# Convolution taps taken in turns over two channel halves, and a new order for all five engines

## The chip, the cores and the metric

One core of one Trainium2 chip runs the whole program. The metric is the device time in microseconds (us) of one execution; of several runs the median is taken. Names used below: PE is TensorE's matmul (PEld its weight load), DVE is VectorE, ACT is ScalarE, POOL is GpSimd, SP is SyncE, which issues most DMAs here.

## The reference

Two layers over 256 tokens of width 1024, float32. Each layer normalises `x`, multiplies it by one wide input matrix, and feeds three groups whose outputs are joined and multiplied by an output matrix:

```
h = rms_norm(x, norm_g);  z = h @ w_in             # 1024 -> 3612 columns
o_a = fox_attention(q, k, v, f_logit) * silu(f_gate)      # 4 heads, forget bias
y   = a * sigmoid(b)                                       # GLU, 256 channels
y   = causal depthwise conv(y, 31 taps) + conv_b
o_b = (silu(layer_norm(y)) @ w_pw) * silu(c_gate)
o_c = nsa_attention(...) * silu(n_gate)                    # 8 heads, 3 branches
x   = x + concat(o_a, o_b, o_c) @ w_out
```

A final RMSNorm follows. The compressed branch of `nsa_attention` gathers blocks of 32 tokens, adds a position table, and sends them through a small two-layer network. What the change touches directly is the depthwise convolution: for each of 256 channels, 31 shifted copies of the sequence times a weight, summed.

## The kernel before, in words

Every float32 product that matters is split into a high and a low part: `form_hi` (ACT, line 227) rounds a 128x1024 piece of weights to the high part, `form_lo` (DVE, line 235) subtracts to get the low part and frees the raw buffer, whereupon SP may fetch the next piece (`pump`; six raw buffers). One input block of 128 columns, `s(i)`, is 24 matmuls on PE (lines 436 to 438), and two neighbouring blocks share one of two PSUM banks of the pool `z`: a block can only start when the bank's former contents have been read.

The 31 taps of the convolution are shared out. The last 11 (`NV`) are done on DVE by `late_taps`: the first is a multiply with bias (line 547), the other ten are `scalar_tensor_tensor` instructions (line 549) that read a shifted window of the padded input `ypad`, multiply by a per-channel weight and add to `yc`. The 256 channels are two halves of 128, so `yc[:, 0]` and `yc[:, 1]` are separate sums of 256 tokens each. The other 20 taps are matmuls: `glu` writes `ypad` (line 506), POOL sends it to a DRAM buffer and reads it back in the shape for matmuls (`yr`), `taps` (line 519) forms the weights and `conv` (line 529) runs 80 small matmuls into `pcn`; `conv_bias` (line 535) adds them to `yc`.

Names in the order of one layer that the prediction uses:

- `fox_kl` (line 707) writes `fklz`, which reads the PSUM bank of blocks 14 and 15 and feeds `fox_scores` (lines 717 and 718, tile `fs`); `fox_mask` (line 461) and `fox_exp` follow, `fox_norm` (lines 740 and 464, tiles `fsu`, `fP`) scales the rows, and `fox_trans` (line 748, tile `fpt`) transposes them on PE.
- `blocks(0)` and `blocks(1)` (line 818) write `xp` on DVE from the bank of blocks 0 and 1; `compress(0)` and `compress(1)` (line 828, tile `ph`) multiply `xp` by weights `ww` on PE.
- `keys_rope`, `keys_lo` (tile `klz`), `query_rope(0)` (tiles `q0r`, `q0u`) and `query` (tile `qs`) are DVE and ACT work that `scores` (tile `sw`) waits for.
- `fox_qh` and `fox_k0` (lines 681 and 695) are copies on POOL.
- `norms`, `trans`, `pv`, `proj1`, `residual` close a layer.

The order of every engine's instructions is the order of the calls in the text of the kernel: the whole program runs under a manual schedule for SP, PE, POOL, DVE and ACT, so that a call which stands later in the text stands later in the queue of each engine it uses, and an engine takes its queue strictly in order. The same list of calls is used for both layers.

Of the kernel before, what the change touches and what calls it, by code (L numbers as in the profile page):

```python
# [12 lines left out]
ALU = mybir.AluOpType  # L13
# [116 lines left out]
def trunk(ctx, tc, a, out, dbg=None):  # L130
# [243 lines left out]
    for l in range(L):  # L374
# [163 lines left out]

            ve.tensor_scalar(S("ct"), S("ct"), 0.5, None, op0=ALU.mult)

        def late_taps(i, a_, b_):

            ctv = S("ct").rearrange("p (i k) -> p i k", i=2)
            for k in range(a_, min(b_, NV)):
                y, w_ = ypad[:, i, 31 - NV + k:31 - NV + k + 256], ctv[:, i, k:k + 1]
                if k == 0:
                    ve.tensor_scalar(yc[:, i], y, w_, S("cb")[:, i:i + 1], op0=ALU.mult, op1=ALU.add)
                else:
# [612 lines left out]
            mprod(1, "A", NA)  # L1161
            a_out(1)
        form_hi()
        form_hi()
        form_lo()
        form_hi()
        form_lo()
        form_lo()
        mprod(1, "B", NB)
        b_out(1)  # L1170
        branch_gates()
        s(2)
        triangle()
        form_hi()
        form_lo()
        half_taps()
        s(3)
        glu_tanh(0)
        glu(0)
        forget()  # L1180
        form_hi()
        form_hi()
        late_taps(0, 0, 2)
        late_taps(0, 2, 4)
        late_taps(0, 4, 6)
        s(4)
        s(5)
        form_lo()
        form_lo()
        s(12)  # L1190
        forget_sum()
        cumulate()
        form_hi()
        form_lo()
        form_hi()
        s(13)
        glu_tanh(1)
        late_taps(0, 6, 8)
        glu(1)
        bias_rows()  # L1200
        late_taps(0, 8, 10)
        form_hi()
        form_hi()
        form_lo()
        form_lo()
        bias_heads()
        fox_q()
        s(14)
        s(15)
        fox_k()  # L1210
        s(6)
        form_lo()
        fox_qh()
        s(7)
        fox_k0()
        late_taps(0, 10, 12)
        late_taps(1, 0, 2)
        late_taps(1, 2, 4)
        form_hi()
        form_lo()  # L1220
        fox_kl()
        form_hi()
        form_lo()
        form_hi()
        form_lo()
        load_w2()
        keys_rope()
        fox_scores(0)
        fox_mask(0)
        form_hi()  # L1230
        form_lo()
        form_hi()
        taps(0)
        fox_scores(1)
        fox_scores(2)
        fox_mask(1)
        s(0)
        late_taps(1, 4, 6)
        s(1)
        fox_exp(0)  # L1240
        fox_exp(1)
        fox_scores(3)
        fox_mask(2)
        blocks(0)
        keys_hi()
        fox_exp(2)
        form_lo()
        s(8)
        taps(1)
        fox_mask(3)  # L1250
        s(9)
        fox_norm(0)
        keys_lo(0)
        query_rope(0)
        keys_lo(1)
        fox_exp(3)
        compress(0)
        part(0)
        blocks(1)
        conv(0)  # L1260
        conv(1)
        query(0, 0)
        compress(1)
        query(0, 1)
        fox_trans(0, 0)
        fox_trans(0, 1)
        fox_copy(0, 0)
        s(10)
        fox_norm(1)
        fox_trans(1, 0)  # L1270
        fox_copy(0, 1)
        late_taps(1, 6, 8)
        late_taps(1, 8, 10)
        late_taps(1, 10, 12)
        form_hi()
        form_lo()
        form_hi()
        form_lo()
        fox_trans(1, 1)
        scores(0)  # L1280
        mask(0, 0)
        part(1)
        fox_copy(1, 0)
        hidden()
        fox_copy(1, 1)
        fox_pv()
        s(11)
        mask(0, 1)
        expo(0, 0)
        expo(0, 1)  # L1290
        conv_bias(0)
        hidden_in()
        conv_bias(1)
        coeff(0)
        norms(0, 0)
        trans(0, 0)
        gelu()
        ln_trans()
        form_hi()
        form_hi()  # L1300
        form_hi()
        norms(0, 1)
        form_hi()
        form_hi()
        form_lo()
        query_rope(1)
        form_lo()
        scores(1)
        compressed_kv()
        compressed_v()  # L1310
        query(1, 0)
        query(1, 1)
        s(16)
        s(17)
        form_hi()
        mask(1, 0)
# [7 lines left out]
        trans(0, 1)
        form_lo()
        ln_norm()
        scores(2)
        mask(2, 0)
        expo(1, 1)
        coeff(1)  # L1330
        norms(1, 0)
        mask(2, 1)
        ptcopy(0)
        gate_tanh(0)
        scores(3)
        gate_mul(0)
        norms(1, 1)
        mask(3, 0)
        expo(2, 0)
        expo(2, 1)  # L1340
        coeff(2)
        norms(2, 0)
        norms(2, 1)
        compressed()
        form_lo()
        form_lo()
        s(19)
        s(20)
        gate_tanh(1)
        trans(1, 0)  # L1350
        trans(1, 1)
        ptcopy(1)
        expo(3, 0)
        scores(4, (0,))
        mask(3, 1)
        mask(4, 0)
        scores(4, (1,))
        mask(4, 1)
        ln_back()
        trans(2, 0)  # L1360
        s(21)
        expo(3, 1)
        scores(5, (0,))
        swish_in()
        trans(2, 1)
        ptcopy(2)
        cmp_scores(0)
        expo(4, 0)
        mixed(0, 2, fx["o"], 0.5)
        expo(4, 1)  # L1370
        gate_mul(1)
        swish()
        cmp_soft(0)
        scores(5, (1,))
        s(22)
        mask(5, 0)
        expo(5, 0)
        mask(5, 1)
        form_hi()
        form_hi()  # L1380
        form_lo()
        coeff(3)
        form_lo()
        norms(3, 0)
        norms(3, 1)
        pointwise()
        s(23)
        cmp_norm(0)
        coeff(4)
        trans(3, 0)  # L1390
        trans(3, 1)
        gate_tanh(2)
        gate_mul(2)
        scores(6, (0,))
        scores(6, (1,))
        scores(7, (0,))
        mix_hi(0, 2)
        mix_lo(0, 2)
        expo(5, 1)
        norms(4, 0)  # L1400
        norms(4, 1)
        ptcopy(3)
        pv(0)
        mask(6, 0)
        pv(1)
        coeff(5)
        pv(2)
        pv(3)
        gate_tanh(3)
        gate_mul(3)  # L1410
        scores(7, (1,))
        form_hi()
        form_hi()
        form_hi()
        cmp_scores(1)
        mixed(2, 2, ln["o"], 0.25)
        cmp_trans(0)
        cmp_copy(0)
        norms(5, 0)
        norms(5, 1)  # L1420
        proj0(0, (0, 1))
        form_lo()
        mix_hi(2, 2)
        mix_lo(2, 2)
        form_lo()
        trans(4, 0)
        ptcopy(4, 0)
        mask(6, 1)
        pv_cmp(0)
        trans(4, 1)  # L1430
        ptcopy(4, 1)
        proj0(0, (2, 3))
        mixed(4, 4, on[0], 0.5, TA)
        mix_hi(4, 4, TA)
        form_lo()
        load_g(a["norm_g"][1] if l == 0 else a["final_g"], nm("gn"))
        expo(6, 0)
        form_hi()
        mix_lo(4, 4, TA)
        trans(5, 0)  # L1440
        trans(5, 1)
        cmp_soft(1)
        proj0(0, (4, 5))
        proj0(0, (6, 7))
        form_lo()
        proj0(1, (0, 1))
        residual(0, 0, 512, pj[0])
        expo(6, 1)
        coeff(6)
        norms(6, 0)  # L1450
        norms(6, 1)
        ptcopy(5, 0)
        ptcopy(5, 1)
        mask(7, 0)
        proj1(range(4))
        form_hi()
        form_hi()
        mask(7, 1)
        expo(7, 0)
        expo(7, 1)  # L1460
        trans(6, 0)
        ptcopy(6, 0)
        trans(6, 1)
        ptcopy(6, 1)
        form_lo()
        form_lo()
        proj0(1, (2, 3))
        proj0(1, (4, 5))
        cmp_norm(1)
        cmp_trans(1)  # L1470
        form_lo()
        cmp_copy(1)
        proj0(1, (6, 7))
        coeff(7)
        norms(7, 0)
        norms(7, 1)
        trans(7, 0)
        ptcopy(7, 0)
        trans(7, 1)
        ptcopy(7, 1)  # L1480
        pv(4)
        pv(5)
        pv(6)
        pv(7)
        residual(0, 512, 512, pj[1])
        nxt.squares(0)
        nxt.rms(0)
        form_hi()
        pv_cmp(1)
        mixed(4, 2, on[1][:, 0:2], 0.5, TB)  # L1490
        form_lo()
        form_lo()
        mix_hi(4, 2, TB)
        mixed(6, 2, on[1][:, 2:4], 0.5, TB)
        mix_hi(6, 2, TB)
        mix_lo(4, 2, TB)
        mix_lo(6, 2, TB)
        proj2(0)
        proj1(range(4, 8))
        form_hi()  # L1500
# [79 lines left out]
```

## Time and profile before

| | us |
|---|---|
| runs | 308.85, 309.65, 310.14 (median 309.65) |
| profiled execution, own time | 308.64 |
| its span, first to last instruction | 306.9 |
| PE busy | 293.0 (95%) |
| DVE busy | 259.8 (85%) |
| ACT busy | 186.2 (61%) |
| POOL busy | 27.5 (9%) |

The profiled execution's own time is 1.7 us longer than its span: that is what lies before the first and after the last instruction. Its time is 1.0 us below the median. The granted clock of PE is full from the first matmul to the last. PE's busy share is the union of matmul spans; matmuls overlap one another, so the share tells that PE always had something under way, and waits show where a matmul starts later than the one before it allows. The last matmul starts at about 299 us; the rest is the final norm and the store.

### The profile page before, as it was taken

The page shows a single profiled execution, that of the slowest core. Times are in us where ns is not written, and L with a number is a line of the kernel's source. Part 1 is how long each engine was busy: PE and PEld are TensorE (multiplying, and loading weights), DVE is VectorE, ACT ScalarE, POOL GpSimd, SP SyncE. Part 2 cuts the span into 40 slices and gives each one's busy share as a digit, 9 for nine tenths or more (in the row PEclk, how much of TensorE's full clock was granted, in tenths as well). Part 3 has the DMA queues.
Part 4 walks back from the last instruction along what each step waited for, and adds up shares of the span by engine and source line. Part 5 has one row for each costly group of instructions (what it writes and reads, how often), then busy time and mean ns, then how long its engine had stood idle before and what let it go on. Part 6 is the DMA issues. An engine that isn't in the chain of part 4 may idle for free.

```text
span 306.9 us, 6505 instructions
## 1 busy us (share of the span) xinstructions
PE 293.0 (95%) x2477; PEld 268.7 (88%) x2477; DVE 259.8 (85%) x676; ACT 186.2 (61%) x408; POOL 27.5 (9%) x53
## 2 busy tenths in 40 slices
PE   8999999998999999999999999999899999999990
PEld 6799999985999998888899999997599999888990
DVE  3947989999999999994874798999999999999443
ACT  4744968182787697673346496727378669776211
POOL 2000343000002000000000030700000200000001
PEclk9999999999999999999999999999999999999997
DMA  7788778748934324543460869774884332230011
GB/s 288 273 329 289 218 256 221 233 164 295 348 108 148 100 85 123 186 156 94 137 231 13 302 194 276 238 260 143 312 308 130 144 115 88 77 137 1 2 68 69
DMA packets 16543, 54.93 MB, mean 179 GB/s; under 512 B 2048, under 2 KB 2560, under 8 KB 16512
## 3 DMA queue, kind: packets, MB, share of 16 engines
q1 hardware_dynamic: 15264, 51.42, 48.5%
q0 software_dynamic: 960, 2.82, 3.5%
q8 instruction: 19, 0.31, 0.4%
q10 hardware_dynamic: 288, 0.28, 0.3%
q14 instruction: 12, 0.10, 0.1%
HBM read 52.88 MB, written 1.64 MB: 178 GB/s over the span
## 4 chain that ended last, share of the span: by engine, by line
PE 73%; DVE 13%; issue 7%; ACT 2%; DMA 2%; POOLq 0%; SPq 0%; POOL 0%; DVEq 0%
PE ps L436 10%; PE ps L438 10%; PE ps L437 10%; PE pA L407 4%; PE pw L1049 4%; PE pw L1052 4%; PE pw L1048 4%; PE pB L407 4%; DVE yc L549 3%; PE pt L967 3%; PE pcn L529 3%; DVE wS_1l L235 3%; DVE wS_0l L235 3%; PE ph L828 2%; PE on L993 2%
## 5 line engine op out<-in xcount | busy, mean ns | idle before, releaser
L436 PE MATMUL ps<-hTh,wS_0h 128*128 128x256 f32 x192 | 54.3, 283 | 0.1
L436 PE MATMUL ps<-hTh,wS_1h 128*128 128x256 f32 x192 | 54.3, 283 | 0.1
L437 PE MATMUL ps<-hTl,wS_0h 128*128 128x256 f32 x192 | 53.6, 279 | 0.0
L437 PE MATMUL ps<-hTl,wS_1h 128*128 128x256 f32 x192 | 53.6, 279 | 0.0
L438 PE MATMUL ps<-hTh,wS_1l 128*128 128x256 f32 x192 | 53.6, 279 | 0.0
L438 PE MATMUL ps<-hTh,wS_0l 128*128 128x256 f32 x192 | 53.6, 279 | 0.0
L436 PEld LDWEIGHTS ps<-hTh,wS_1h 128*128 128x128 f32 x192 | 36.1, 188 | 0.5 <-PE ps L438 0.3
L436 PEld LDWEIGHTS ps<-hTh,wS_0h 128*128 128x128 f32 x192 | 36.1, 188 | 0.5 <-PE ps L438 0.3
L437 PEld LDWEIGHTS ps<-hTl,wS_0h 128*128 128x128 f32 x192 | 36.1, 188 | 0.1
L437 PEld LDWEIGHTS ps<-hTl,wS_1h 128*128 128x128 f32 x192 | 36.1, 188 | 0.1
L438 PEld LDWEIGHTS ps<-hTh,wS_0l 128*128 128x128 f32 x192 | 36.1, 188 | 0.0
L438 PEld LDWEIGHTS ps<-hTh,wS_1l 128*128 128x128 f32 x192 | 36.1, 188 | 0.0
L235 DVE TENSOR_TENSOR wS_1l<-wS,wS_1h 128x1024 fp32r<-128x1024 f32 x24 | 29.0, 1238 | 3.7 <-ACT wS_1h L227 3.6
L937 ACT ACTIVATE P<-P,mx 128x128 f32<-128x128 f32 (+1 forms) x64 | 28.5, 447 | 5.9 <-DVE mx L461 5.9
L235 DVE TENSOR_TENSOR wS_0l<-wS,wS_0h 128x1024 fp32r<-128x1024 f32 x24 | 29.0, 1238 | 0.9 <-ACT wS_0h L227 0.8
L227 ACT CAST wS_0h<-wS 128x1024 fp32r<-128x1024 f32 x24 | 23.8, 1048 | 8.0 <-DMA wS<-in_wS 7.9
L227 ACT CAST wS_1h<-wS 128x1024 fp32r<-128x1024 f32 x24 | 23.8, 1048 | 7.8 <-DMA wS<-in_wS 7.8
L549 DVE SCALAR_TENSOR_TENSOR yc<-ypad,sm,yc 128x256 f32<-128x256 f32 x40 | 20.3, 507 | 1.1
L979 ACT COPY PT<-pt 128x512 f32<-128x512 f32 x24 | 13.4, 584 | 10.2 <-PE pt L967 10.2
L461 DVE CUSTOM_DVE_ANT_0 P<-sw,cf 128x128 f32<-128x128 f32 (+1 forms) x64 | 19.3, 352 | 0.1
L464 DVE TENSOR_SCALAR P<-P,co 128x128 f32<-128x128 f32 (+1 forms) x64 | 16.4, 315 | 0.0
L967 PE MATMUL pt<-cf,P 128*128 128x128 f32 x96 | 14.0, 272 | 0.0
(242 smaller groups left out, 676.8 us busy)
## 6 DMA issues: line engine op xcount, KB each, us to landing
wS<-in_wS SPq DMA_DIRECT2D x48, 512.0 KB, 5.1
ww<-in_w SPq DMA_DIRECT2D x16, 512.0 KB, 4.0
wO<-in_wo SPq DMA_DIRECT2D x16, 512.0 KB, 3.7
yr<-ybuf POOLq DMA_DIRECT2D x16, 136.0 KB, 4.9
wA<-in_wA SPq DMA_DIRECT2D x4, 420.0 KB, 4.6
wB<-in_wB SPq DMA_DIRECT2D x4, 390.0 KB, 5.3
x<-in_x SPq DMA_DIRECT2D x2, 512.0 KB, 3.9
w<-in_w SPq DMA_DIRECT2D x2, 448.0 KB, 5.6
```

What stands on the lines that cost most here:

```text
L227: sc.copy(hi, w)
L235: ve.tensor_tensor(lo, w, hi.bitcast(F32), op=ALU.subtract)
L407: te.matmul(p[:, :n], a_[:, k, tok], b_, start=first, stop=s_ == "t" and k == 7)
L436: te.matmul(o, hi[:, k], hTh[:, k], start=k == 0, stop=False)
L437: te.matmul(o, hi[:, k], hTl[:, k], start=False, stop=False)
L438: te.matmul(o, lo[:, k], hTh[:, k], start=False, stop=k == 7)
L461: ve.tensor_tensor_reduce(o, x, m, -1.0, 3.0e38, ALU.add, ALU.min, mx)
L464: ve.tensor_scalar(x, x, r, None, op0=ALU.mult)
L549: ve.scalar_tensor_tensor(yc[:, i], y, w_, yc[:, i], op0=ALU.mult, op1=ALU.add)
L937: sc.activation(Ps[n][:, g, b], Ps[n][:, g, b], AF.Exp, bias=mxs[n][:, c:c + 1], scale=-1.0, accum_out=sus[n][:, c:c + 1])
L967: te.transpose(pts[n][:, o + b * 128:o + (b + 1) * 128], Pg[:, b * 128:(b + 1) * 128], C("id"))
L979: sc.copy(PT, pts[n, g])
```

## The change

`late_taps` loses its argument for the half: for each tap it now emits one instruction for half 0 and one for half 1, so that two instructions in a row write different sums. Before, the 11 taps of half 0 were emitted in groups of two, then those of half 1.

```
-        def late_taps(i, a_, b_):
+        def late_taps(a_, b_):
...
             for k in range(a_, min(b_, NV)):
-                y, w_ = ypad[:, i, 31 - NV + k:31 - NV + k + 256], ctv[:, i, k:k + 1]
-                if k == 0:
...
-                    ve.scalar_tensor_tensor(yc[:, i], y, w_, yc[:, i], op0=ALU.mult, op1=ALU.add)
+                for i in range(2):
+                    y, w_ = ypad[:, i, 31 - NV + k:31 - NV + k + 256], ctv[:, i, k:k + 1]
+                    if k == 0:
...
+                        ve.scalar_tensor_tensor(yc[:, i], y, w_, yc[:, i], op0=ALU.mult, op1=ALU.add)
```

The second part is the list of calls of a layer, some 350 lines, which is written in another order. The instructions are the same in number and kind on every engine; lines below 546 are one higher in the new kernel. Two lines of the list as an example:

```
-        late_taps(0, 0, 2)
...
+        late_taps(0, 1)
```

On DVE in the first layer, in the old order, between the row sums of the first two heads (`fsu_0_760`, `fP_0_758`) and the second block of `xp` (`xp_0_964`) stood the keys' low parts and the first query rotation:

```order
L740 RECIPROCAL fsu_0_760<-fsu_0_760 128x4
L464 TENSOR_SCALAR fP_0_758<-fP_0_758,fsu_0_760 128x128
L464 TENSOR_SCALAR fP_0_758<-fP_0_758,fsu_0_760 128x256
...
L780 TENSOR_TENSOR klz_119<-ku_748,kh_0_857 64x512
L453 STREAM_SHUFFLE q0r_927<-ps_0_866 128x512
L454 TENSOR_TENSOR q0u_928<-ps_0_866,cf 128x512
L455 TENSOR_TENSOR q0r_927<-q0r_927,cf 128x512
L456 TENSOR_TENSOR q0u_928<-q0u_928,q0r_927 128x512
L780 TENSOR_TENSOR klz_120<-ku_748,kh_0_858 64x512
L818 TENSOR_TENSOR xp_0_964<-ps_0_786,sm_88 64x16x15 x4
```

In the new order, the same place (`fsu_0_793` and `fP_0_791` are the same heads, `xp_0_915` the second block, `fP_0_931` the mask of the third head):

```order
L550 SCALAR_TENSOR_TENSOR yc_133<-ypad_134,sm_88,yc_133 128x256 x4
L235 TENSOR_TENSOR wS_0l<-wS_0_734,wS_0h 128x1024
L741 RECIPROCAL fsu_0_793<-fsu_0_793 128x4
L464 TENSOR_SCALAR fP_0_791<-fP_0_791,fsu_0_793 128x128
L464 TENSOR_SCALAR fP_0_791<-fP_0_791,fsu_0_793 128x256
...
L819 TENSOR_TENSOR xp_0_915<-ps_0_740,sm_88 64x16x15 x4
L461 ISA fP_0_931,fmx_0_932<-fs_0_822,cf 128x128
```

The second `xp` now follows the row scaling at once; the mask of the third head, the rotation, both `klz` and the mask of the fourth head come behind it. Between `fklz` and this place stand 14 taps instead of two.

On PE in the old order, from the convolution's matmuls (`pcn`) on, the transposes of the first two heads (`fpt_0_1041`, `fpt_0_1045`) came after both `compress`, and an input block before those of the last two:

```order
L529 MATMUL pcn_970<-yr_0_570,cw_772 32x256 x20
L828 MATMUL ph_0_1014<-ww_1_0_0_767,xp_0_964 32x256 x4
...
L828 MATMUL ph_0_1014<-ww_1_3_0_948,xp_0_964 32x256 x4
L748 MATMUL fpt_0_1041<-cf,fP_0_758 128x128 x3
L748 MATMUL fpt_0_1045<-cf,fP_0_758 128x128 x3
L436 MATMUL ps_0_1051<-hTh,wS_0h 128x256
...
L748 MATMUL fpt_0_1081<-cf,fP_0_846 128x128 x3
```

In the new order (`fpt_0_921`, `fpt_0_925` are the first two heads, `fpt_0_1066` the third, `sw_0_1061` the first `scores`):

```order
L749 MATMUL fpt_0_921<-cf,fP_0_791 128x128 x3
L749 MATMUL fpt_0_925<-cf,fP_0_791 128x128 x3
L829 MATMUL ph_0_936<-ww_0_0_0_632,xp_0_892 32x256 x4
...
L529 MATMUL pcn_971<-yr_0_477,cw_588 32x256 x20
L529 MATMUL pcn_971<-yr_0_529,cw_588 32x256 x20
L829 MATMUL ph_0_1019<-ww_1_0_0_830,xp_0_915 32x256 x4
...
L908 MATMUL sw_0_1061<-kh_0_888,qs_0_963 128x256
...
L749 MATMUL fpt_0_1066<-cf,fP_0_931 128x128 x3
```

The transposes of the first two heads now stand ahead of `compress(0)`, and those of the third and fourth follow `compress(1)` with only one `scores` of four matmuls between. In the last part of the layer, `pv(4)` and `pv(5)` stand ahead of `trans(6, 0)` instead of behind `trans(7, 1)`, and the first half of `proj1` behind the last `pv` instead of ahead of it.

## Rows read from the trace of the kernel before

**Rows 1.** Waits of PE: line waited for, us in total, times, longest.
```profile
PE ph L828 <- issue: 3.0, 2, 1.5
PE fs L718 <- DVE fklz L707: 0.8, 2, 0.4
```

**Rows 2.** Windows: stretch, its us, busy us of each engine, PE's clock, DMA.
```profile
76.00:140.00 64.00, 63.91 (x486) 58.85 (x486) 61.71 (x201) 48.21 (x120) 1.63 (x1) 1.00 0.48 160
```

**Rows 3.** Timeline of PE around `fox_scores`: start us, us, instruction.
```profile
51.56 0.22 PE L717 MATMUL fs<-fk,fq 128*128 128x128 f32 x1
53.37 0.22 PE L717 MATMUL fs<-fk,fq 128*128 128x128 f32 x1
53.83 0.28 PE L436 MATMUL ps<-hTh,wS_0h 128*128 128x256 f32 x1
```

**Rows 4.** Timeline of PE around `compress`.
```profile
65.60 1.93 PE L828 MATMUL ph<-ww,xp 128*32 128x256 f32 x32
67.35 4.50 PE L529 MATMUL pcn<-yr,cw 128*32 128x256 f32 x80
73.34 1.93 PE L828 MATMUL ph<-ww,xp 128*32 128x256 f32 x32 [1.50 <-issue]
75.21 0.87 PE L748 MATMUL fpt<-cf,fP 128*128 128x128 f32 x6
78.76 0.82 PE L748 MATMUL fpt<-cf,fP 128*128 128x128 f32 x6
79.33 0.36 PE L907 MATMUL sw<-kh,qs 128*128 128x256 f32 x1
79.89 1.02 PE L848 MATMUL hidT<-cf,part 128*128 128x32 f32 x8
```

**Rows 5.** Timeline of DVE over the same stretch.
```profile
66.48 0.17 DVE L740 RECIPROCAL fsu<-fsu 128x4 f32<-128x4 f32 x1
66.69 1.01 DVE L464 TENSOR_SCALAR fP<-fP,fsu 128x128 f32<-128x128 f32 x4
67.61 0.68 DVE L780 TENSOR_TENSOR klz<-ku,kh 64x512 fp32r<-64x512 f32 x1
71.58 1.66 DVE L818 TENSOR_TENSOR xp<-ps,sm 64x240 f32<-64x240 f32 x4
73.27 1.39 DVE L796 SCALAR_TENSOR_TENSOR qs<-q0u,qs 64x512 fp32r<-64x512 f32 x2
```

**Rows 6.** Timeline of DVE at two groups of taps.
```profile
29.29 0.42 DVE L506 SCALAR_TENSOR_TENSOR ypad<-th,ps 128x256 f32<-128x256 f32 x1 [2.05 <-ACT th L502]
30.20 2.57 DVE L549 SCALAR_TENSOR_TENSOR yc<-ypad,sm,yc 128x256 f32<-128x256 f32 x5
32.69 1.22 DVE L235 TENSOR_TENSOR wS_0l<-wS,wS_0h 128x1024 fp32r<-128x1024 f32 x1
60.77 1.00 DVE L549 SCALAR_TENSOR_TENSOR yc<-ypad,sm,yc 128x256 f32<-128x256 f32 x2
61.68 0.28 DVE L461 CUSTOM_DVE_ANT_0 fP<-fs,cf 128x128 f32<-128x128 f32 x1
62.24 1.66 DVE L818 TENSOR_TENSOR xp<-ps,sm 64x240 f32<-64x240 f32 x4
```

**Rows 7.** Timeline of POOL, then of DVE, 45 to 53 us.
```profile
46.15 2.36 POOL L695 CAST fklz<-cLR 64x512 fp32r<-64x512 f32 x2
...
45.66 1.62 DVE L235 TENSOR_TENSOR wS_0l<-wS,wS_0h 128x1024 fp32r<-128x1024 f32 x1
50.14 1.22 DVE L235 TENSOR_TENSOR wS_0l<-wS,wS_0h 128x1024 fp32r<-128x1024 f32 x1
51.39 1.41 DVE L707 TENSOR_TENSOR fklz<-ps,fk 64x512 fp32r<-64x512 f32 x2
```

**Rows 8.** End of the first layer: timeline of DVE, then of PE.
```profile
138.97 1.14 DVE L464 TENSOR_SCALAR P<-P,co 128x256 f32<-128x256 f32 x4
...
139.97 1.04 PE L967 MATMUL pt<-cf,P 128*128 128x128 f32 x8
```

More of the change, by code (lines that the diff above doesn't have):

```diff
@@ L1163, in trunk @@
         form_hi()
+        half_taps()
+        form_lo()
+        mprod(1, "B", NB)
+        s(2)
+        form_hi()
+        form_lo()
+        form_hi()
+        s(3)
+        b_out(1)
+        forget()
+        form_lo()
+        triangle()
+        form_hi()
+        form_hi()
+        form_hi()
+        forget_sum()
+        form_lo()
+        form_lo()
+        cumulate()
+        s(4)
+        bias_rows()
+        form_hi()
+        glu_tanh(0)
+        glu(0)
+        s(5)
+        glu_tanh(1)
@@ new lines, in trunk @@
+        form_lo()
+        form_lo()
+        form_hi()
+        branch_gates()
+        form_hi()
+        form_hi()
+        glu(1)
+        late_taps(0, 1)
+        form_lo()
+        s(12)
+        s(13)
+        taps(0)
+        late_taps(1, 2)
+        bias_heads()
+        form_hi()
+        s(14)
+        fox_k0()
+        late_taps(2, 3)
+        taps(1)
+        form_lo()
+        fox_q()
+        form_lo()
+        form_lo()
+        form_hi()
+        form_hi()
+        s(15)
+        s(6)
@@ new lines, in trunk @@
+        blocks(0)
+        form_hi()
+        late_taps(8, 9)
+        late_taps(9, 10)
+        form_lo()
+        fox_exp(1)
+        fox_norm(0)
+        blocks(1)
+        fox_trans(0, 0)
+        fox_trans(0, 1)
+        fox_copy(0, 0)
+        fox_mask(2)
+        compress(0)
+        part(0)
+        query_rope(0)
+        conv(0)
+        conv(1)
+        keys_lo(0)
+        keys_lo(1)
+        fox_mask(3)
+        compress(1)
+        query(0, 0)
+        query(0, 1)
+        fox_exp(2)
@@ new lines, in trunk @@
+        fox_exp(3)
+        late_taps(10, 11)
+        conv_bias(0)
+        part(1)
+        fox_norm(1)
+        scores(0)
+        fox_trans(1, 0)
+        fox_copy(0, 1)
+        conv_bias(1)
+        load_w2()
+        fox_trans(1, 1)
+        fox_copy(1, 0)
+        fox_copy(1, 1)
+        mask(0, 0)
+        form_hi()
+        scores(1)
+        mask(0, 1)
+        mask(1, 0)
+        mask(1, 1)
+        form_hi()
+        form_hi()
+        hidden()
+        form_hi()
+        form_lo()
@@ new lines, in trunk @@
+        norms(1, 1)
+        gate_tanh(0)
+        compressed_kv()
+        scores(2)
+        mask(2, 0)
+        mask(2, 1)
+        ptcopy(0)
+        ln_stats()
+        compressed_v()
+        form_hi()
+        form_hi()
+        expo(2, 0)
+        gate_mul(0)
+        scores(3)
+        trans(1, 0)
+        trans(1, 1)
+        s(18)
+        scores(4, (0,))
+        expo(2, 1)
+        ptcopy(1)
+        form_hi()
+        form_hi()
+        form_hi()
+        form_lo()
+        form_lo()
@@ new lines, in trunk @@
+        form_lo()
+        mask(3, 0)
+        load_g(a["norm_g"][1] if l == 0 else a["final_g"], nm("gn"))
+        expo(3, 0)
+        mask(3, 1)
+        mixed(0, 2, fx["o"], 0.5)
+        expo(3, 1)
+        mask(4, 0)
+        coeff(2)
+        norms(2, 0)
+        norms(2, 1)
+        ln_norm()
+        s(19)
+        s(20)
+        s(21)
+        gate_tanh(1)
+        form_hi()
+        compressed()
+        ln_back()
+        form_lo()
+        trans(2, 0)
+        gate_mul(1)
+        trans(2, 1)
@@ new lines, in trunk @@
+        scores(4, (1,))
+        swish_in()
+        ptcopy(2)
+        coeff(3)
+        swish()
+        scores(5, (0,))
+        scores(5, (1,))
+        form_hi()
+        cmp_scores(0)
+        mask(4, 1)
+        expo(4, 0)
+        s(22)
+        expo(4, 1)
+        norms(3, 0)
+        mask(5, 0)
+        cmp_soft(0)
+        form_hi()
+        pointwise()
+        coeff(4)
+        scores(6, (0,))
+        scores(6, (1,))
+        norms(3, 1)
+        norms(4, 0)
+        gate_tanh(2)
@@ new lines, in trunk @@
+        expo(5, 0)
+        trans(3, 0)
+        trans(3, 1)
+        s(23)
+        mix_hi(0, 2)
+        cmp_norm(0)
+        ptcopy(3)
+        cmp_trans(0)
+        mask(5, 1)
+        gate_mul(2)
+        expo(5, 1)
+        scores(7, (0,))
+        form_lo()
+        mask(6, 0)
+        mixed(2, 2, ln["o"], 0.25)
+        expo(6, 0)
+        mask(6, 1)
+        scores(7, (1,))
+        pv(0)
+        pv(1)
+        cmp_copy(0)
+        form_lo()
+        form_lo()
+        form_hi()
+        gate_tanh(3)
@@ L1164, in trunk @@
+        nxt.squares(0)
+        mix_hi(4, 2, TB)
+        mixed(6, 2, on[1][:, 2:4], 0.5, TB)
+        mix_lo(4, 2, TB)
+        mix_hi(6, 2, TB)
+        proj1(range(4))
+        mix_lo(6, 2, TB)
+        proj1(range(4, 8))
+        proj2(0)
+        form_hi()
         form_hi()
@@ L1324, in trunk @@
[L1324 to L1344, printed above, removed]
+        nx_trans_lo()
+        res1()
+        res2(0)
+        proj2(1)
+        res2(1)
```

448 lines of the change are left out of this document (128 added, 320 removed).

## Prediction

> **What bounds the kernel now.** I read the waits of PE first, then the windows, then the timelines of PE and DVE side by side. PE is busy for 293.0 of 306.9 us and its clock is full, so the count of matmuls, which the change leaves as it is, sets most of the time; a new order can only take away waits of PE, or add some. The reader is to see that PE waits long in two places per layer: before `compress(1)`, 1.50 us each time, and in `fox_scores` for `fklz`, 0.4 us each time [rows 1]. The first is called "issue", because no release was recorded. The timelines name it: the second `xp` starts at 71.58 us on DVE, takes 1.66, so ends at 73.24, and PE goes on at 73.34 [rows 4, 5]. DVE is late at both places. In `fox_scores` the loss is larger than the one wait: three heads take from 51.56 to 53.83, 2.27 us, while the third alone takes 0.46; three of these are 1.38, so 0.89 us are lost [rows 3]. Together 0.89 + 1.50 = 2.4 us per layer, 4.8 in both, that DVE makes PE wait. From 76 to 140 us neither has much left: PE 63.9 and DVE 61.7 of 64 us [rows 2]. So DVE is the second bound, and what counts is when it reaches the instruction PE waits for.
>
> **The change part by part.**
>
> *The taps.* Five taps of one half in a row start at 30.20, and the next other instruction at 32.69: 2.49 us [rows 6]. Two in a row go from 60.77 to 61.68: 0.91 us [rows 6]. The pair has one step from a tap to the tap that adds to the same sum, the five have four such steps; with a the step to an unrelated instruction and b the step to a dependent tap, a + b = 0.91 and a + 4b = 2.49, so b = 0.53 and a = 0.38; I take 0.52 and 0.40, so 0.12 us for each dependent step. In the new order the two halves alternate and no tap reads what the instruction just before it wrote. The trace of before does not show a tap that reads the sum written two instructions earlier; its price is bounded by 0.40 (nothing waits: the one before the last started 0.8 us earlier, and a pair lasts 1.00 in all) and 0.52 (as the dependent one). I take 0.40. A layer has 15 such steps before (five groups with 5, 1, 1, 3 and 1 of them ahead of the second `xp`, 4 behind), so 1.8 us of DVE per layer, 3.6 in both, of which 1.3 lie ahead of the second `xp`. That is no gain by itself: it counts only where PE waits.
>
> The Trainium skill speaks against this part: "VectorE: DVE Perf Modes", section "The DRAIN you can't avoid", says that a VectorE instruction does not start until the pipeline of the one before is empty, and that a chain with a semaphore after each instruction took as long as one without. By it alternating would save nothing; the rows above differ by 0.12 us a step, so the trace does not agree, and I give the rule a rival below.
>
> *The stretch up to the second `xp`.* Behind it now stand the mask of the third head and that of the fourth (0.56 each: 61.68 to 62.24 [rows 6]), and both `klz` with the rotation between them (67.61 to 71.58, 3.97 [rows 5]): 5.09 us moved. Ahead of it stand 20 taps instead of 17. The 17 cost, group by group, 6 x 0.52 or so and the rest: 2.94 + 0.91 + 0.91 + 2.29 + 0.91 = 7.96 without disturbance; the 20 cost 8.0 at 0.40. So the taps cancel. The disturbance is POOL's: while it copied `cLR` into `fklz` for 2.36 us, a subtraction of 1.22 us took 1.62, and from 45.66 to 50.14 one subtraction and five taps took 4.48 us instead of 1.2 + 2.29, so about 1.0 us was lost [rows 7]. The copies are still there in the new order, in another place; their cost is bounded by 0 (no DVE instruction with two inputs in SBUF beside them) and 2.0 (both kinds of copies disturb); I leave it at 1.0, as the row has it. The idle 2.05 us that DVE spent waiting for the first `glu` [rows 6] is bounded by 0 and 2.05 in the new order, which puts other work there (four low parts and the chain of the forget bias), but waits for ACT's `tanh` and for the matmuls of `cumulate` in its place; I take 0.9 recovered. Then the second `xp` ends at 73.24 - 5.09 - 0.9 = 67.3 us.
>
> *`fklz`.* It ended at 52.80 (51.39 + 1.41 [rows 7]). Ahead of it stand six taps instead of 15 (2.4 for 7.05), two more low parts (2.4), and both `cw` (1.5, an estimate by their 128x640 elements against the 128x1024 of a 1.22 us subtraction); with 0.9 recovered it ends at 52.80 - 4.65 + 3.9 - 0.9 = 51.15. PE now needs it at the next input block, which shares the bank, at 51.56 [rows 3]: in time, by 0.4 us. If it is late, block 0 and everything behind it on PE wait.
>
> *The transposes of `fox`.* Without the 0.89 us PE reaches this place at 65.60 - 0.89 = 64.7 [rows 4]. `fpt` now comes first there. Its input is ready one `xp` (1.66) and one head's scaling (0.46, half of 66.69 to 67.61 [rows 5]) before 67.3, at 65.2: a new wait of about 0.6 us. `compress(0)`, `conv`, `compress(1)` run through behind it, for `xp` is done: the 1.50 us go. Then `scores(0)` and the third head's `fpt`. For that DVE must, after 67.3, do a mask (0.56), rotation and `klz` (3.97), a mask (0.56), `qs` (1.39 [rows 5]), two taps and one `conv_bias` (3 x 0.40), the reciprocal (0.21) and the first head (0.46): 8.35 us, so 75.65, and PE goes on at 75.7. PE alone would be there at 64.7 + 9.61 (65.60 to 75.21) - 1.50 + 0.87 + 0.56 = 74.2 [rows 4]. So here PE waits again, about 1.5 us less the 0.6 it has waited before. Before, PE was at this `fpt` at 78.76, with the same work done but one input block more (75.21 + 0.87 to 78.76: 2.7) and one `scores` less (79.33 to 79.89: 0.56): 76.6 in the new order's terms. The gain is 76.6 - 75.7 = 0.9; I take 0.8, rounded towards nothing because `fklz` has so little room. Bounds: if DVE recovers all of the 2.05 and loses nothing to POOL, PE is alone the limit, 76.6 - 74.2 = 2.4; if nothing is recovered and POOL costs double, 0.9 - 0.9 - 1.0 = -1.0, a loss.
>
> *The rest of the layer.* DVE saves another 0.5 (four dependent steps). The last transposes started at 139.97, with the rows scaled from 138.97 on [rows 8]: PE follows DVE here by under half a us. In the new order `pv(4)` and `pv(5)` stand ahead and half of `proj1` behind, which on balance asks the rows of DVE earlier, and `residual(0, 0)` (0.7) leaves DVE's way too. I put this at zero: bounds are the gain handed back (-0.8) and another 0.5.
>
> *The end.* The final norm hangs on the last matmuls as before. Zero.
>
> *Sum.* 0.8 x 2 layers = 1.6 us. Against the profiled execution's 308.64 that is 307.0; the median of the runs is 1.0 higher than that execution, so 308.0.
>
> **The rivals.**
>
> 1. *DVE is no longer late at all.* Both waits go and no new one comes: 2.4 x 2 = 4.8 us, 304.8. For it: the taps ahead of `fklz` fall from 15 to 6. Against it: `fpt` asked for right behind `compress(1)` needs 8.35 us of DVE in a stretch where PE has 9.6 - 1.5, and DVE is full there.
>
> 2. *The waits only move.* What is won at `compress(1)` is lost at the two `fpt` and at the end of the layer, where DVE and PE run 0.5 us apart: 309.6, within 1 us. For it: rows 2 and 8.
>
> 3. *Slower: `fpt` blocks PE's queue.* PE takes its queue in order, so `compress`, `conv` and `scores` now stand behind transposes that wait for DVE. If DVE reaches the third head's scaling later than 76.6 instead of 75.65, each further us is lost by PE in full. POOL's copies beside the four low parts that now stand in a row before `fklz`, at twice the price, with nothing of the 2.05 recovered, would do it: 1.0 us loss per layer, 308.0 + 1.6 + 2.0 = 311.6. It decides from 0.95 us lateness on.
>
> 4. *The taps get no cheaper.* The 22 taps ahead of the third head cost 0.12 more each, 2.6 us, DVE reaches it at 78.3, PE loses 1.7 a layer: 313.0. The rule of the skill named above would lead here; the rows on two and five taps speak against it.
>
> **How the numbers follow.** The forecast 0.38 (307 to 309), rival 1 0.15, rival 2 0.30, rival 3 0.13, rival 4 0.04. A measurement of this kernel can tell about 0.5%, 1.55 us, from no change. Faster than 308.1: some 0.6 of the forecast, rival 1, and a little of rival 2: 0.43. Slower than 311.2: most of rivals 3 and 4, a little of 2: 0.17. The same: 0.40. The range that holds 8 in 10 is 305.2 to 311.3; the forecast's own is 307 to 309.
>
> **What would show it.** In the profile after: taps that start 0.40 us apart, else rival 4. `compress(1)` following `conv` with no idle time; a wait of 0.3 to 1 us ahead of the first `fpt` and of about 1 us ahead of the third, both released by the scaling on DVE. If PE stands at neither, rival 1; if the third `fpt` waits over 2 us, rival 3. `fs` without a wait for `fklz`, and the first matmul of block 0 within 0.3 us of block 7's last. The forecast is wrong if PE's waits per layer sum to under 1 or over 3 us, or if a new wait stands after 100 us.

## The result, and the profile after

The kernel after takes 307.62 us (median of 6 runs, 307.23 to 307.67); in the same comparison the kernel before takes 309.09 (6 runs, 308.48 to 310.14). The ratio is 0.9945, with a 95% interval of 0.9929 to 0.996. The profiled execution of after takes 307.66 us, its span is 305.9: 1.0 us less than the 308.64 and 306.9 of before. So the forecast of 308.0 came true, but as the rest shows, not by the terms that it added up.

The waits of PE in the kernel after (line waited for, us in total, times, longest), to be held against [rows 1]:

```profile
PE fpt L749 <- DVE fP L464: 1.3, 2, 0.7
PE ph L829 <- DMA ww<-in_w: 0.5, 1, 0.5
```

Neither wait of before is left. DVE is now waited for at `fpt`, and once a transfer is. The timeline of PE around `compress` in the first layer, against [rows 4]:

```profile
64.58 1.14 PE L749 MATMUL fpt<-cf,fP 128*128 128x128 f32 x6
65.65 1.93 PE L829 MATMUL ph<-ww,xp 128*32 128x256 f32 x32
67.64 4.52 PE L529 MATMUL pcn<-yr,cw 128*32 128x256 f32 x80
71.97 1.91 PE L829 MATMUL ph<-ww,xp 128*32 128x256 f32 x32
75.23 1.16 PE L749 MATMUL fpt<-cf,fP 128*128 128x128 f32 x6 [0.68 <-DVE fP L464]
```

`compress(1)` follows `conv` at 71.97. The six transposes at 64.58 take 1.14 us where six take 0.87 in [rows 4]: their operand becomes ready piece by piece. The third `fpt` waits. The timeline of DVE over the same stretch, against [rows 5 to 7]:

```profile
48.89 1.41 DVE L708 TENSOR_TENSOR fklz<-ps,fk 64x512 fp32r<-64x512 f32 x2
61.29 1.67 DVE L550 SCALAR_TENSOR_TENSOR yc<-ypad,sm,yc 128x256 f32<-128x256 f32 x4
62.88 1.22 DVE L235 TENSOR_TENSOR wS_0l<-wS,wS_0h 128x1024 fp32r<-128x1024 f32 x1
64.22 1.01 DVE L464 TENSOR_SCALAR fP<-fP,fsu 128x128 f32<-128x128 f32 x4
65.26 1.66 DVE L819 TENSOR_TENSOR xp<-ps,sm 64x240 f32<-64x240 f32 x4
74.89 1.01 DVE L464 TENSOR_SCALAR fP<-fP,fsu 128x128 f32<-128x128 f32 x4
```

The second `xp` ends at 66.92 instead of 73.24; four alternating taps take 61.29 to 62.88, 0.40 each. The second layer, PE:

```profile
209.89 1.16 PE L749 MATMUL fpt<-cf,fP 128*128 128x128 f32 x6 [0.60 <-DVE fP L464]
217.31 1.48 PE L829 MATMUL ph<-ww,xp 128*32 128x256 f32 x24
219.30 0.64 PE L829 MATMUL ph<-ww,xp 128*32 128x256 f32 x8 [0.51 <-DMA ww<-in_w]
```

Here the first `fpt` waits longer, and the last quarter of `compress(1)` waits for its weights. And the end, PE and DVE, first of before (the last matmuls, the last residual):

```profile
298.34 1.10 PE L1052 MATMUL pw<-wO_1h,hTl 128*128 128x256 f32 x8
...
300.19 0.42 DVE L1055 TENSOR_TENSOR x<-pw,x 128x256 f32<-128x256 f32 x1
```

and of after:

```profile
297.81 1.10 PE L1053 MATMUL pw<-wO_1h,hTl 128*128 128x256 f32 x8
...
298.95 0.42 DVE L1056 TENSOR_TENSOR x<-pw,x 128x256 f32<-128x256 f32 x1 [1.29 <-PE pw L1053]
```

Before, the last residual starts 0.75 us after the last matmul ends (299.44); after, 0.04.

From 76 to 140 us, against [rows 2] (windows):

```profile
76.00:140.00 64.00, 64.00 (x519) 58.94 (x520) 59.88 (x196) 46.62 (x119) 0.72 (x1) 1.00 0.49 164
```

DVE is busy for 1.8 us less there than before.

The books of PE: the distance of each matmul's start from the start of the one ahead of it, added up from the two traces by what the matmul writes, in us, before and after (differences of 0.15 and more; those ahead of the first input block, which cancel, are left out).

| | layer 0 | change | layer 1 | change |
|---|---|---|---|---|
| `ph` (`compress`) | 5.19, 3.48 | -1.71 | 5.21, 4.20 | -1.01 |
| `fs` | 2.74, 1.85 | -0.89 | 2.66, 1.85 | -0.81 |
| `fpt` | 1.58, 2.83 | +1.25 | 1.57, 2.90 | +1.32 |
| `sw` (`scores`) | 5.26, 5.78 | +0.53 | 5.26, 5.78 | +0.52 |
| `on` (`pv`, `pv_cmp`) | 7.63, 7.99 | +0.35 | 7.64, 7.99 | +0.36 |
| `pcn`, `pkv` | 5.16, 5.60 | +0.44 | 5.16, 5.60 | +0.44 |
| `ps` (input blocks) | 68.11, 67.55 | -0.56 | 68.11, 67.56 | -0.55 |

With the small ones the first layer gains 0.6 us, the second loses 0.1, and the last matmul starts 0.54 earlier (299.17, 298.64). The rest of the 1.0 is the end: 0.71 at the last residual, of which the output's transfer gives 0.2 back.

### The profile page after: what moved, and what is told of

Read it like the earlier page. It is cut to its first block, busy times and chain, and to the rows that moved or that the text cites. A ratio compares the mean times of both kernels' runs of the same rounds, so it can differ in the third digit from the quotient of the medians.

```text
span 305.9 us, 6520 instructions
## 1 busy us (share of the span) xinstructions
PE 295.1 (96%) x2477; PEld 268.0 (88%) x2477; DVE 257.0 (84%) x676; ACT 185.2 (61%) x408; POOL 24.5 (8%) x53
## 4 chain that ended last, share of the span: by engine, by line
PE 56%; DVE 23%; ACT 8%; issue 7%; DMA 4%; POOLq 0%; SPq 0%; POOL 0%
PE ps L436 6%; PE ps L438 6%; PE ps L437 6%; DVE yc L550 5%; PE pA L407 4%; DVE wS_1l L235 4%; PE on L994 4%; PE pw L1049 4%; PE pw L1050 4%; PE pw L1053 4%; PE pt L968 4%; DVE wS_0l L235 3%; DMA ww<-in_w 2%; PE sw L908 2%; PE pB L407 2%
## 5 line engine op out<-in xcount | busy, mean ns | idle before, releaser
L550 DVE SCALAR_TENSOR_TENSOR yc<-ypad,sm,yc 128x256 f32<-128x256 f32 x40 | 18.3, 514 | 0.2
L737 ACT ACTIVATE fP<-fP,fmx 128x128 f32<-128x128 f32 (+1 forms) x16 | 7.1, 445 | 15.7 <-DVE fmx L461 15.7
```

## The experiments

Theory A: DVE's time up to the third `fpt` sets when PE goes on, so the alternating taps and the order each give only what lets DVE come earlier there. Rival B: the order alone did it. Times are medians; ratios are of the means, to the runs of before on the same chip.

**e1, the order without the turns.** In the kernel after:

```
-    for k in range(a_, min(b_, NV)):
-        for i in range(2):
+    for n in range(2 * a_, 2 * min(b_, NV)):
+        i, k = divmod(n, NV)
```

> The kernel after with the order of all engines as it is, but the 22 taps of a layer fill the same places with half 0 first and half 1 behind it, so that 14 taps of a layer read the sum that the VectorE instruction just before them wrote (none in the kernel after). Theory A (VectorE's arrival at the third head's scaling sets TensorE there, one for one, and the alternating taps supply some of it): 13 of the 14 dependent steps lie ahead of that scaling, 13 x 0.12 = 1.6 us later per layer, so the third fpt waits 2.2 to 2.5 us instead of 0.8 and the time is 307.6 + 2 x 1.5 = 310.6 (309.9 to 311.2). Rival B (the searched order alone gives the gain, the taps' sequence is worth nothing): 307.6, within 0.4, and taps 0.40 us apart.

Measured: 310.36 us, ratio 1.0026 (1.0012 to 1.004). The whole gain of the change is gone, and more. The waits of PE, then five taps of half 0 and the next instruction on DVE:

```profile
PE fpt L749 <- DVE fP L464: 4.5, 4, 1.5
```

```profile
51.68 2.60 DVE L550 SCALAR_TENSOR_TENSOR yc<-ypad,sm,yc 128x256 f32<-128x256 f32 x5
54.19 0.41 DVE L548 TENSOR_SCALAR yc<-ypad,sm 128x256 f32<-128x256 f32 x1
```

Five taps take 2.51 us. In PE's books `fpt` rises by 1.76 and 1.67 per layer against the kernel after; over 13 dependent steps that is 0.13 each. Theory A holds, B falls; only the place differs, for the wait stands at the first and the third `fpt`, and not at the third alone.

**e2, the turns where the old order admits them.** In the kernel before:

```
-        late_taps(0, 8, 10)
+        turns((0, 8), (1, 0))
...
-        late_taps(0, 10, 12)
-        late_taps(1, 0, 2)
-        late_taps(1, 2, 4)
+        turns((1, 1), (0, 9), (1, 2), (0, 10), (1, 3))
```

> The kernel before with its order, in which only the sequence of seven taps is changed so that the halves alternate from the place on where both are there: 11 dependent steps per layer instead of 15, the four that go lie ahead of the subtraction for fklz. Theory A: 4 x 0.12 = 0.5 us per layer earlier at fklz and at the second xp, so TensorE's wait before compress(1) falls from 1.5 to 1.0 and the one for fklz below 0.2; in all 1.0 us: 308.1 (307.8 to 308.6) where before has 309.1. Rival B (only the order counts): 309.1, within 0.3.

Measured: 308.83 us, ratio 0.9982 (0.9967 to 0.9996): 0.55 us, about half of what A said. The timeline of POOL, then of DVE, tells why:

```profile
48.10 1.39 POOL L685 CAST cLh<-fq 64x512 fp32r<-64x512 f32 x2
49.44 1.56 POOL L699 CAST fklz<-cLR 64x512 fp32r<-64x512 f32 x2
...
47.41 3.86 DVE L553 SCALAR_TENSOR_TENSOR yc<-ypad,sm,yc 128x256 f32<-128x256 f32 x5
51.20 1.21 DVE L235 TENSOR_TENSOR wS_0l<-wS,wS_0h 128x1024 fp32r<-128x1024 f32 x1
```

Beside POOL's copies each of the five takes 0.76 us though none is a dependent step, so in this layer the steps saved there bought nothing: the first `fpt` comes 52.32 us after the layer's first input block, for 52.13 in the kernel before. In the second layer only one tap runs beside the copies, and there it comes at 51.54 for 52.06, the 0.5 us that A had.

**e3, the end of before in the kernel after.** In the last layer only:

```
-        proj1(range(4, 8))
-        proj2(0)
+        if last: proj2(0); proj1(range(4, 8))
+        else:    proj1(range(4, 8)); proj2(0)
```

> The kernel after, with the second half of proj1 of the last layer put back behind the first half of proj2, as in the kernel before. Theory A (part of the gain comes at the end: before, VectorE reached the last residual 0.7 us after the last matmul, because the residual of the other half and its norm came late; after, it waits for the last matmul): the last residual starts 0.6 to 0.8 us after the last matmul's end again, 308.2 to 308.5. Rival C (the end is set by the last matmuls and the output's transfer in both, as the prediction had it): 307.6, within 0.3.

Measured: 308.47 us, ratio 0.9965 (0.9951 to 0.998), 0.6 us slower than after by the ratios. PE's last matmuls and DVE's last residual:

```profile
297.82 1.11 PE L1053 MATMUL pw<-wO_1h,hTl 128*128 128x256 f32 x8
...
299.67 0.42 DVE L1056 TENSOR_TENSOR x<-pw,x 128x256 f32<-128x256 f32 x1
```

The last matmuls stand where they stood, the residual comes 0.74 us behind their end. A holds for the end. This run also tells what the late `ww` cost. With the same order up to there its last quarter landed at 217.30 instead of 219.25, and PE did not wait for it, but then waited for DVE. The third `fpt` of the second layer, after and e3:

```profile
220.57 1.16 PE L749 MATMUL fpt<-cf,fP 128*128 128x128 f32 x6
...
220.58 1.16 PE L749 MATMUL fpt<-cf,fP 128*128 128x128 f32 x6 [0.69 <-DVE fP L464]
```

It starts at the same time in both, so the late `ww` cost nothing: DVE sets this place. What makes the second layer of after longer than the first is seen in the six taps behind `fklz` on DVE, first layer and second:

```profile
50.33 2.85 DVE L550 SCALAR_TENSOR_TENSOR yc<-ypad,sm,yc 128x256 f32<-128x256 f32 x6
...
194.99 3.53 DVE L550 SCALAR_TENSOR_TENSOR yc<-ypad,sm,yc 128x256 f32<-128x256 f32 x6
```

In the first layer one of them runs beside POOL's copies and takes 0.75 us, in the second three do, and the others 0.40. That is 0.7 us, and the third `fpt` comes 52.19 us after the first input block of the first layer and 52.97 after that of the second. In e3, with one such tap in either layer, it comes at 52.17 and 52.28.

**e4, two moves against the waits that are left, badly made.** In the kernel after:

```
         blocks(1)
-        fox_trans(0, 0); fox_trans(0, 1); fox_copy(0, 0)
         fox_mask(2); compress(0); part(0); query_rope(0); conv(0); conv(1)
+        fox_trans(0, 0); fox_trans(0, 1); fox_copy(0, 0)
...
+        fox_norm(1)
         late_taps(10, 11); conv_bias(0); part(1)
-        fox_norm(1)
```

> The kernel after with two moves: on VectorE the scaling of the second pair of heads stands ahead of the last two taps and the first conv_bias (1.2 us), and on TensorE the first two fpt stand behind compress(0) and conv instead of ahead of them. Theory A (TensorE's waits at the first and the third fpt are what is left of the change's room, and nothing behind takes them over at once): the first fpt loses 0.3 and 0.9 us less in the two layers, the third 0.8 and 0.1 less, a new wait of 0.5 before scores(1) for its bank, which conv_bias(1) frees; in all 1.0 to 1.9 us less: 305.7 to 306.6. Rival D (VectorE is full through to the end of the layer, so that a wait that goes here comes back at the next masks): 307.6, within 0.4, with TensorE waits between 76 and 100 us that the kernel after hasn't. In both the transfer of the fourth ww stays late in the second layer (0.9 us).

Measured: 315.08 us, ratio 1.0136 (1.0092 to 1.0179). Both theories missed. ACT, then PE:

```profile
72.44 0.48 ACT L753 COPY fPT<-fpt 128x384 f32<-128x384 f32 x1 [5.09 <-PE fpt L749]
...
78.07 1.07 PE L749 MATMUL fpt<-cf,fP 128*128 128x128 f32 x6 [1.23 <-DVE fP L464]
```

I had moved the copy of `fpt` on ACT too. ACT takes its queue in order, so it stood idle for 5.09 us in front of that copy, with the copies into `kh`, those for `qs` and the exponentials behind it. Of the 7.1 us that the profiled execution (314.72) lost against after, some 2.5 came by a lower clock in the first layer (last section).

**e5 and e6, the two moves with the transposes and their copy further ahead.** Both now stand ahead of `conv` and `query_rope`; e4 with its copy alone put right was not tried. e5 is this alone:

```
         blocks(1)
-        fox_trans(0, 0); fox_trans(0, 1); fox_copy(0, 0)
         fox_mask(2); compress(0); part(0)
+        fox_trans(0, 0); fox_trans(0, 1); fox_copy(0, 0)
         query_rope(0)
```

> The kernel after; on TensorE the first two fpt go behind compress(0), and on ScalarE the copy of the first one goes behind part(0) only, ahead of the copies that klz and qs need. Theory A (VectorE's lateness at the two fpt is what the new order pays; the one at the first can be filled by compress(0), which needs nothing that is late): the first fpt waits for nothing, 0.3 us less in the first layer and 0.9 in the second; the start of conv, 0.2 late after part(0), comes free of that as well. In the first layer the third fpt waits longer by as much, since VectorE sets it; in the second, where the fourth ww is late by 0.9, that transfer starts earlier with compress(0). In all 0.3 to 1.2 us less: 306.5 to 307.4. Rival D (VectorE alone sets the time up to the third fpt, so TensorE's own order there is worth nothing): 307.6, within 0.3.

e6 has the move of `fox_norm(1)` as well:

> As e5_fpt_behind_compress, and on VectorE the scaling of the second pair of heads stands ahead of the last two taps and the first conv_bias, 1.2 us earlier. Theory A: the third fpt waits for nothing any more (0.8 in the first layer of the kernel after), and scores(1) waits about 0.5 for the bank that conv_bias(1) frees; against e5_fpt_behind_compress 0.4 to 0.8 us less per layer, in all 304.8 to 306.4. Rival D: the waits move on to scores(1) and the next masks, so the time is that of e5_fpt_behind_compress, within 0.3.

Measured: e5 308.24 us, ratio 0.9959 (0.993 to 0.9989), no better than after. Its executions spread from 306.3 to 312.3 us; the six whose mean granted clock is 0.993 or more have a median of 306.9, as A had it, and the others lose more to the clock (last section). But these six were picked after the fact, and the trace speaks for D. PE's wait for the third `fpt` has grown:

```profile
PE fpt L749 <- DVE fP L464: 2.4, 2, 1.2
```

In PE's books of the profiled execution (306.92) the first layer changes by only 0.1 us: `pcn` saves 0.23, `fpt` takes 0.39. The second is 0.9 shorter than that of after, but in it one tap runs beside POOL's copies where after has three, which is worth 0.7 (e3).

e6 305.27 us, ratio 0.9866 (0.9845 to 0.9887; 4 runs), below both kernels. Its PE in the first layer:

```profile
66.83 0.87 PE L749 MATMUL fpt<-cf,fP 128*128 128x128 f32 x6
67.63 4.52 PE L529 MATMUL pcn<-yr,cw 128*32 128x256 f32 x80
74.51 1.07 PE L749 MATMUL fpt<-cf,fP 128*128 128x128 f32 x6
75.33 0.36 PE L908 MATMUL sw<-kh,qs 128*128 128x256 f32 x1
```

Nothing waits here any more, and from its first input block to that of the next this layer takes 143.26 us for 144.55 in after, with one tap beside the copies in both. The wait before `scores(1)` that I had put in the sum did not come: it starts at 75.33, ahead of both `conv_bias` (75.79), so in this order its bank is not one that they free.

**e9, the scaling alone.** In the kernel after, only the move of `fox_norm(1)`.

> The kernel after with one move alone: on VectorE the scaling of the second pair of heads ahead of the last two taps and the first conv_bias; TensorE's order as it was. Theory A (what is left of TensorE's waits in the kernel after is VectorE's lateness at each fpt by itself): the third fpt waits for nothing, 1.0 to 1.3 us less per layer, the first fpt waits as before (0.3 and 0.9): between the kernel after (307.6) and both moves together (305.3), at 306.0 to 306.6. Rival (only both moves together work, as fpt behind compress(0) alone left the time within its spread): 307.2 to 307.7.

Measured: 308.02 us, ratio 0.9962 (0.9937 to 0.9986). That is above both ranges; the rival is right that the move alone gives nothing. PE's waits:

```profile
PE sw L908 <- DVE yc L535: 2.1, 2, 1.1
PE fpt L749 <- DVE fP L464: 0.4, 1, 0.4
```

The third `fpt` is free, and the same time is lost just behind it at `scores(1)`, for the bank that `conv_bias(1)` frees. So by the medians this move alone gives nothing, the other nothing either, and both 2.4; how much of that is the other bank was not tried apart.

**e10, the turns taken out of the best version.** The edit of e1, in e6.

> The kernel e6_both_moves, with the taps of half 0 first and those of half 1 behind, in the same places: 13 dependent steps ahead of the scaling of the first pair. Theory A (VectorE is just in time there, so that each dependent step comes back in TensorE's waits): VectorE is 13 x 0.12 = 1.6 us later per layer, TensorE waits at scores(0) for qs and at the third fpt, 305.3 + 3.0 = 308.3 (307.6 to 308.8). Rival B (without the waits VectorE has room, the sequence of the taps no longer counts): 305.3, within 0.5.

Measured: 307.89 us, ratio 0.9979 (0.9947 to 1.001), within A's range. PE waits at the first of the two places that A named, and not at the third `fpt`:

```profile
PE sw L908 <- DVE qs L797: 2.2, 4, 0.9
```

The profile is of an execution that also lost clock (311.33, last section). By the medians the turns are worth 2.6 us here, as 2.7 in the kernel after; without the four executions that lost clock it is 2.4.

**e11, the second `xp` earlier, alone.** In the kernel before:

```
         fox_norm(0)
+        blocks(1)
         keys_lo(0); query_rope(0); keys_lo(1); fox_exp(3); compress(0); part(0)
-        blocks(1)
```

> The kernel before with one move alone: the second xp (blocks(1)) goes on VectorE ahead of both klz and the rotation between them, 3.97 us earlier; taps and all other orders as they were. Theory A (the wait before compress(1), 1.5 us per layer, is only VectorE's order there, and needs neither the alternating taps nor the search): compress(1) follows conv at once, and the third fpt, behind an input block, finds its rows scaled since 75.1: 1.0 to 1.5 us less per layer, 306.2 to 307.3 where before has 309.3. Rival D (the wait moves on to the next place where VectorE is late, since VectorE has the same work up to there): 308.7 to 309.5, with a new wait at scores(0), at an fpt or in the input blocks behind.

Measured: 309.60 us, ratio 1.0007 (0.9993 to 1.0021); rival D. The wait before `compress(1)` is gone (`ph` -1.70 and -1.51 in PE's books) and stands elsewhere:

```profile
PE ps L436 <- DVE sg L477: 2.2, 2, 1.1
PE pt L967 <- DVE P L464: 0.7, 2, 0.5
```

**e8, POOL's copies on ACT.** In the kernel before, `gp.tensor_copy` becomes `sc.copy` in `fox_qh` and `fox_k0`.

> The kernel before with its order and taps, in which the four copies into cLh and fklz are done by ScalarE instead of GpSimd. Theory F (GpSimd's copies slow VectorE's two-input instructions beside them, a tap from 0.40 to 0.75 us, and that is 1.0 us per layer ahead of fklz; a tap beside them costs the same whether it is dependent or not, which is why the alternating taps alone gave half of what the dependent steps were worth): VectorE reaches fklz and the second xp 1.0 us earlier, so TensorE waits 0.9 less for fklz and before compress(1): 309.1 - 2 x 0.9 = 307.3 (306.7 to 308.2). Rival G (the copies cost VectorE nothing there, or ScalarE, which does them later behind its casts, gives the time back): 309.1 to 310.0.

Measured: 310.48 us, ratio 1.0045 (1.0028 to 1.0063); rival G. ACT, then DVE:

```profile
48.63 1.26 ACT L695 CAST fklz<-cLR 64x512 fp32r<-64x512 f32 x2
...
47.93 1.53 DVE L549 SCALAR_TENSOR_TENSOR yc<-ypad,sm,yc 128x256 f32<-128x256 f32 x3
50.88 1.23 DVE L235 TENSOR_TENSOR wS_0l<-wS,wS_0h 128x1024 fp32r<-128x1024 f32 x1 [1.41 <-ACT wS_0h L227]
```

The taps run undisturbed (in this trace no step of one is longer than 0.52 us, but for the wait shown), so F is right on the contention; but DVE then idles 1.41 us for the cast that ACT makes later.

**e7, `pv(4)` and `pv(5)` beside `pv(6)`**, in the kernel after:

```
-        pv(4); pv(5)
...
+        pv(4); pv(5)
         pv(6)
```

> The kernel after with pv(4) and pv(5) put back beside pv(6), as the kernel before has them. Theory E (each change of TensorE between a full-width matmul and a column tile costs 0.1 to 0.2 us, and the new order has one such group more per layer, which gives back 0.35 us of what the waits gave): 307.6 - 0.7 = 306.9 (306.7 to 307.2). Rival: pv(4) and pv(5) fill a wait for VectorE where they stand, and nothing is gained or up to 0.5 us is lost: 307.6 to 308.1.

Measured: 309.47 us, ratio 1.0006 (0.9988 to 1.0024), 1.9 us slower than after by the ratios; the rival, at a higher price than it said. PE's waits:

```profile
PE ptc L1031 <- DVE pcm L1027: 1.3, 2, 0.6
PE pt L968 <- ACT PT L980: 0.5, 2, 0.2
```

The two had filled waits for DVE and ACT of 1.2 us per layer (`ptc` +0.8, `pt` +0.4); the change of tile gave back only 0.15.

**e12, the new end in the kernel before**, in both layers:

```
-        proj2(0); proj1(range(4, 8))
+        proj1(range(4, 8)); proj2(0)
```

> The kernel before with one move alone, in both layers: the second half of proj1 ahead of the first half of proj2, as the kernel after has it. Theory A (the last residual waited for VectorE, which had the other half's residual and norm to do late; e3_old_end was 0.6 to 0.9 slower than the kernel after by that): the last residual follows the last matmul, 0.6 to 0.8 us less, 308.4 to 308.8 where before has 309.3. Rival C (the end is the output's transfer, which varies by some tenths): 309.3, within 0.3.

Measured: 312.82 us, ratio 1.0116 (1.0088 to 1.0144), a loss that neither had. The waits of PE, then the end:

```profile
PE pw L1048 <- ACT hTh L485: 2.9, 3, 1.0
```

```profile
303.67 1.10 PE L1052 MATMUL pw<-wO_1h,hTl 128*128 128x256 f32 x8
...
304.81 0.42 DVE L1055 TENSOR_TENSOR x<-pw,x 128x256 f32<-128x256 f32 x1 [1.29 <-PE pw L1052]
```

At the end A is right again, 0.04 us. But in before's order the second half of `proj1` stands right behind `mix_hi`, which ACT has not made, and PE waits three times in two layers. From 146 to 152 us, where two of these waits stand, the granted clock was 0.75 on average, so part of the loss is the clock's. In before's order the new end does not pay.

## Why the prediction was right, and where it was not

- *What bounds the kernel*: right that DVE is the second bound. But I read the wait before `compress(1)` as a place to be repaired; e11 repaired it alone and gained nothing. It was where a shortage of DVE time showed.
- *The taps*: 0.40 and 0.12 per dependent step came true (0.40 in the rows, 0.13 by e1). "So the taps cancel" and "it counts only where PE waits" undersold them: without the turns the new order gains nothing (e1). The rule of the Trainium skill, "VectorE: DVE Perf Modes", section "The DRAIN you can't avoid", as the prediction reads it, would have e1 as fast as the kernel after; the runs differ by 2.5 us by the ratios. The section also says that an instruction that is not held starts earlier, which the prediction left out.
- *Up to the second `xp`*: 66.92 for 67.3. DVE was busy 25.88 us from 20 to 50 us, for 25.06 before, so 0.8 recovered for 0.9. POOL's price was too high in this layer: one tap of 0.75 us, some 0.4 instead of 1.0, and none of it ahead of `fklz`, which ended at 50.30 for 51.15. In the second layer it was right, with three taps of 0.75, 1.05.
- *The transposes*: in the first layer `fpt` rose by 1.25 us for the 1.5 I had, and the third waits for DVE at 75.23 for my 75.7. In the second the first one waits 0.6, as forecast for both.
- *The term that failed*: "the rest of the layer", put at zero. It cost 0.75 us in the first layer and about as much in the second (`sw`, `on`, `pcn`, `pkv` +1.3, `ps` -0.6). Most of it is other neighbours for PE's groups: the first four `sw` matmuls take 0.47 us behind transposes before and 0.77 behind `compress` after; 0.2 of it is a late start of `conv`, which goes in e5 and e6. So the waits gave 1.35 us in the first layer (-1.71 - 0.89 + 1.25), more than the 0.8 forecast, and 0.6 was left. In the second layer DVE reached the third `fpt` 0.8 later, 0.7 of it by the two more taps beside POOL's copies, and nothing was left: per layer 0.6 and -0.1 for 0.8 and 0.8. That the late `ww` stands in the second layer's books (`ph` 4.20 for 3.48) changes nothing, as DVE would have held PE as long (e3).
- *The end*, put at zero, gave 0.71. "The final norm hangs on the last matmuls as before" was wrong: before, it hung on DVE (e3, e12).
- *The offset*: I added 1.0 from the profiled execution to the median; the profiled execution of after stands at its median (307.66, 307.62), and of the 1.0 half was the draw of three runs, for six give before 309.09. This error and that of the end offset the layers' 1.1 us; the sum came out by luck.
- *The rivals*: of waits that only move the half is true in the kernel after, and e9 and e11 are that case in full. Of my own signs, PE's waits per layer within 1 to 3 us held in the second layer (0.60 and 0.51); in the first the profile lists 0.68, under the bound, and it takes the 0.3 at the first `fpt` and the 0.2 at `conv` to come over 1. "No new wait after 100 us" holds for the first layer only, since `ww` was late at 219.

## What to carry to other kernels

Where a second engine is nearly full, a wait in the timeline names the place where its shortage shows, and moving its work about only moves the wait; first take time from that engine, then order it. Here the order without the turns gained nothing (e1), and four of the turns without the order 0.55 us (e2). Before moving an instruction, list what it issues on every engine's queue: in e4 ACT stood idle for 5 us in front of a copy that went along with the transposes. Read the last instructions behind the last matmul by themselves, for there a late engine counts in full.

## What the runs showed of the hardware

A tap that adds to a sum written two instructions earlier starts 0.40 us after the one ahead of it, as an unrelated instruction does; one that reads the sum of the instruction just ahead starts after 0.52. Beside POOL's copies it is 0.75 in either case: three independent taps in a row in after (from 195.39), a dependent one in before (193.22).

A group of matmuls costs more behind a group of another tile shape. Eight `pv_cmp` matmuls take 0.89 us behind transposes (before: 124.17 to 125.06) and 1.00, after a first gap, behind the 64-column `pv` (after):

```profile
120.44 1.16 PE L1039 MATMUL on<-PTc,vbd 128*128 128x128 f32 x8
121.44 0.27 PE L968 MATMUL pt<-cf,P 128*128 128x128 f32 x1
```

In either kernel the first of the eight starts 0.20 us after the last `pv` matmul and the second 0.21 after the first, where 0.11 is the rule behind transposes. The Trainium skill, "TensorEngine Tiling (Array Packing)", section "Key Properties", says that a change of tiling mode drains TensorE; the trace agrees that the change costs time, some 0.2 us here, and does not show whether a drain is the cause.

The granted clock fell in some experiments after PE had waited. Windows of the e4 kernel (stretch, us, busy us of each engine, clock, DMA), in the first layer and in the second:

```profile
72.00:80.00 8.00, 5.53 (x56) 3.80 (x55) 4.29 (x15) 6.75 (x18) 0.00 (x0) 0.97 0.86 313
80.00:90.00 10.00, 10.00 (x62) 10.00 (x62) 6.91 (x27) 6.06 (x17) 0.00 (x0) 0.69 0.67 222
...
225.00:235.00 10.00, 8.07 (x63) 7.50 (x64) 8.70 (x34) 7.60 (x17) 0.00 (x0) 1.00 0.72 280
```

PE was busy for 5.53 of 8 us, then part of the next ten ran at 1.2 instead of 2.4 GHz, and `ps` took 2.5 us longer; in the second layer like waits (`sw` +1.37 and `fpt` +0.31 in PE's books, for +1.34 and +0.38) cost no clock. In e10 the same came and went between executions: eight of twelve took 307.4 to 308.1 us at a mean clock of 0.99 or more, four 310.6 to 311.4 at 0.98. So a wait of PE can cost more than its length; which ones do was not settled.
